# Two small matmul groups on column halves, 512-token projections in the last layer, and a priority for attention tasks in a two-layer hybrid kernel

## The chip, the cores and the metric

The kernel runs on one core of a Trainium2 chip. The metric is the device time of one execution in microseconds. The engines that matter are TensorE (PE; its weight loads are listed as PEld), VectorE (DVE), ScalarE (ACT), GpSimd (POOL) and the queue of SyncE (SP), from which nearly all DMAs are issued.

## The reference

Two layers work on 528 tokens (16 meta tokens ahead of 512 real ones; the reference also has 112 padding rows, which the kernel leaves away). Each layer does:

```
hn   = rmsnorm(h)
proj = hn @ w_in                    # 1024 -> sq sk sv | rq rk rv rg | u
sb   = stick_breaking(sq, sk, sv)   # 6 heads of 64, log-sigmoid and a running sum over the keys
ro   = rmsnorm(retention(rotary(rq), rotary(rk), rv)) * silu(rg)   # 6 heads, chunks of 128, one state
so   = s5_mixer(u)                  # diagonal state space model, then a gated output
h    = h + concat(sb, ro, so) @ w_out
hn   = rmsnorm(h)
h    = h + (silu(hn @ w_gate) * (hn @ w_up)) @ w_down              # 1024 -> 2816 -> 1024
```

Only the 512 real tokens of the last layer are returned. In that layer the meta tokens still act as keys, values and state, but nothing needs their queries (sq, rq) or their gate (rg).

## The kernel before, in words

Activations lie transposed, 128 channels of the partitions by 528 tokens. Every large product is done with operands split into a high and a low part of type fp32r, and three products (high by high, low by high, high by low) added in PSUM. `mm3` (L352) does this: for each of the K tiles of 128 rows and each of the three products one matmul per bank. A PSUM bank takes 512 columns, so 528 tokens go as two banks of 264 columns, and the 512 tokens of the last layer's output projection and MLP (`open_ps`, `spans`) as one bank of 512. The 23 column blocks of `w_in` (three head pairs of each of sq, sk, sv, rq, rk, rv, rg, and two of u) come in the order of the string `PROJ`. In the last layer they are done for all 528 tokens too (`proj`, L1088; `scaled`, L1103, multiplies by the norm on DVE and so empties the banks).

Attention, retention and S5 are small matmuls with long stretches of ACT, DVE and POOL between them. They are written as Python generators, called tasks. `spawn` (L172) puts a task on one list. `mm3` calls `tick` (L191) after each step, and `tick` runs, in the order of the list, up to six tasks whose due time has come and whose resource is free, each up to its next `yield`; a task that has run goes to the end of the list. So the program order of every engine's queue is fixed when the kernel is built. Due times come from `spend` (L96): every operation is charged to its engine by a formula of `Timed` (V, SC and G are DVE, ACT and POOL), for instance 160 + 1.2 x columns ns for a DVE operation with both inputs in SBUF, and a task is due again when its last operation is reckoned done. Waiting tasks hold or wait for resources that are counted in Python too: 6 of the 8 PSUM banks, and 4 of those 6 for attention scores (`take`, `banks`).

- `sb_lane` / `sb_pair` / `sb_group`: stick breaking for one head pair after the other (tiles z, e, sp, hi, lo, av).
- `ret_lane` / `ret_pair` (L955): retention for a head pair: transposes (rtp), the product of keys and values of four chunks (kv), scores (sc), output (ro), then the norm over the head (hsq, hps) and the gate (sg).
- `s5_lane` / `s5_mix` / `s5_glu`: es, scans on DVE, yps, ysm, then the gated product (pj from hi/lo of ysm, glu).
- `s5_params` with `outputs` (L617): builds the matrices of S5, among them the kernel matrix (kps, copied by DVE into tz).
- `Unit.drive`: the split of the next weight block into its two parts (wh on ACT, wl on DVE).

In kv one matmul a chunk forms the 128x128 product of both heads of the pair, of which only the two diagonal 64x64 blocks are read. In kps eight matmuls of two K parts write 32 partitions by 4 x 128 columns.

After the projections the output projection runs in three parts (`OUT_PARTS`): in the first layer stick breaking (mix 0, 1, 2), then S5 (6, 7), then retention (3, 4, 5); in the last layer S5, stick breaking, retention. Ahead of each part `drain` runs tasks alone until the part's inputs are there; inside a part `mm3` ticks the tasks that are left.

Of the kernel before, what the change touches and what calls it, by code (L numbers as in the profile page):

```python
# [12 lines left out]
ALU = mybir.AluOpType  # L13
# [75 lines left out]
def hybrid_kernel(ctx, tc, A, out, dbg=None):  # L89
# [16 lines left out]
    class Timed:  # L106
# [6 lines left out]
        def __getattr__(self, name):  # L113
            f = getattr(self.eng, name)

            def issue(*a, **k):
# [7 lines left out]
                return f(*a, **k)  # L124
            return issue

    V = Timed(nc.vector, "V", {"one": (150, 1.05), "two": (160, 1.2), "tensor_scalar": (150, 0.55),
                               "tensor_tensor_scan": (180, 2.2)})
    SC = Timed(nc.scalar, "SC", {"one": (230, 0.8), "two": (230, 0.8)})
    G = Timed(nc.gpsimd, "G", {"one": (180, 2.1), "two": (180, 2.1), "memset": (100, 0.85)})  # L130
# [1 line left out]
    def mm(out, lhsT, rhs, start, stop, more=False):  # L132

        n = math.prod(out.shape[1:]) / 2.4
        t = 2 * max(109.0, 2 * n + 3) if rhs.dtype == F32 else max(110.0, 1.055 * n + 5)
        spend("PE", t / 2 if 64 in (rhs.shape[0], out.shape[0]) else t)
        nc.tensor.matmul(out, lhsT=lhsT, rhs=rhs, start=start, stop=stop, skip_group_check=more)  # L137
# [31 lines left out]

    tasks = []  # L170

    def spawn(gen, at=0.0):  # L172
        tasks.append([gen, at, None, None, 0.0])

    free = {"bank": BANKS, "scores": ZBANKS, "group": GROUPS}

# [14 lines left out]
    def tick(most=TICKS):  # L191

        done = 0
        for t in list(tasks):
            if done < most and t[1] <= busy["PE"] + LEAD and (t[2] is None or t[2]()):
                tasks.remove(t)
                now[0] = t
                t[3] = None
                try:
                    t[2] = next(t[0])  # L200
                    tasks.append(t)
                except StopIteration:
                    pass
                now[0] = None
                done += 1
        return done
# [139 lines left out]
    def open_ps(nt, s="pj"):  # L346
        return [bank(s), bank(s)] if nt == T else [bank(s)]
# [4 lines left out]
    def mm3(ps, w, x, c0=0, nt=T, first=True, last=True, ticks=TICKS):  # L352

        a, b = w
        xh, xl = x
        kt = len(xh)
        for k in range(kt):
            for i, (wt, xt) in enumerate(((a, xh), (a, xl), (b, xh))):
                for p, (c, n) in zip(ps, spans(nt)):
                    mm(p[:, :n], lhsT=wt[:, k, :], rhs=xt[k][:, c0 + c:c0 + c + n],  # L360
                       start=first and k == 0 and i == 0, stop=last and k == kt - 1 and i == 2)
                tick(ticks)
# [177 lines left out]
    def s5_params(l, engines, scal, par):  # L540
# [76 lines left out]
        def outputs():  # L617

            c_r, c_i = v3(braw[:, 2 * P:3 * P]), v3(braw[:, 3 * P:4 * P])
            for hf in range(2):  # L620
                for ri in range(2):
                    gg[ri, hf] = gp.tile([P, 640], F32, tag="g", name=nm("gg"))
                    G.memset(gg[ri, hf], 0.0)
            for ri in range(2):
                mul, add, sub = on(engines[ri])
                pr, pi = powers(0, 5)
                x1, x2 = (gp.tile([P, 640], F32, tag="g", name=nm("gx")) for _ in range(2))
                mul(v4(x1, 5), wide(c_r, 5), pi if ri else pr)
                mul(v4(x2, 5), wide(c_i, 5), pr if ri else pi)
                yield  # L630
                for q in range(2):
                    r = slice(64 * q, 64 * q + 64)
                    for hf in range(2):
                        o = gg[ri, hf][r, :].rearrange("p (m c) -> p m c", c=32)[:, :, 16 * q:16 * q + 16]
                        a, b = (x[r, 320 * hf:320 * hf + 320].rearrange("p (m c) -> p m c", c=16) for x in (x1, x2))
                        (add if ri else sub)(o, a, b)
                yield
            bbd = [tt("bbd"), tt("bbd")]
            for ri, src in ((0, bbr), (1, bbi)):
                G.memset(bbd[ri][:, :256], 0.0)  # L640
                for q in range(2):
                    engines[ri].tensor_scalar(
                        out=bbd[ri][64 * q:64 * q + 64, :256].rearrange("p (t c) -> p t c", c=32)[:, :, 16 * q:16 * q + 16],
                        in0=src[64 * q:64 * q + 64], scalar1=-1.0 if ri else 1.0, scalar2=None, op0=ALU.mult)
            now[0][1] += 2000 + 10000 * l
            yield
            for hf in range(2):
                yield from banks(1)
                ps = bank("kps")
                for t in range(4):  # L650
                    for ri in range(2):
                        mm(ps[0:32, P * t:P * t + P], lhsT=bbd[ri][:, 32 * (4 * hf + t):32 * (4 * hf + t) + 32],
                           rhs=gg[ri, hf][:, 160 * t:160 * t + P], start=ri == 0, stop=ri == 1)
                tz[hf] = tt("tz")
                G.memset(tz[hf], 0.0)
                yield
                pv = ps.rearrange("p (t c) -> p t c", c=P)
                for j in range(Q):
                    o = tz[hf][96 - 32 * j:128 - 32 * j, :512].rearrange("p (t c) -> p t c", c=P)[:, :, 32 * j:P]
                    V.tensor_copy(out=o, in_=pv[0:32, :, 0:P - 32 * j])  # L660
                yield
                freed(1)
            over.append("outputs")
# [291 lines left out]
    def ret_pair(l, p, q, k, vt, gate, res):  # L955
# [21 lines left out]
        yield from banks(1)  # L977
        ps = bank("kv")
        for j in range(4):
            mm(ps[:, P * j:P * j + P], lhsT=kt[:, P * j:P * j + P], rhs=v[:, P * j:P * j + P], start=True, stop=True)  # L980
        yield
        for hh in range(2):
            r, c = slice(64 * hh, 64 * hh + 64), 64 * hh
# [100 lines left out]
    for l in range(LAYERS):  # L1084
        got = {}
        mix = [None] * 8

        def proj(w):  # L1088
            ps = open_ps(T)
            mm3(ps, w, nrm.x)  # L1090
            return ps

        def two_proj():
# [8 lines left out]

        def scaled(n, ps):  # L1103
            t = tt(n)
            for b, (c, m) in zip(ps, spans(T)):
                V.tensor_tensor(out=t[:, c:c + m], in0=b[:, :m], in1=nrm.rr[:, c:c + m], op=ALU.mult)
            return t

        def after(n, p, t, l=l, got=got, mix=mix):

# [32 lines left out]
            for i in range(2):  # L1143
                mix[6 + i] = yield from slow_split(so[i])

        spawn(s5_lane())
        for p in range(3):
            spawn(sb_lane(p))
        for p in range(3):
            spawn(ret_lane(p))  # L1150
        held = []
        for i, (n, p) in enumerate(proj_order(l)):
            if l == 0 and i < 2:
                if i == 0:
                    first = two_proj()
                held.append((n, p, first[i]))
            else:
                held.append((n, p, proj(weight())))
            if i == HOLD[l]:
                nrm.finish()  # L1160
                if l == 0:
                    spawn(first_params())
            if i >= HOLD[l]:
                for n, p, ps in held:
                    spawn(after(n, p, scaled(n, ps)), busy["V"])
                held = []
        last = l == LAYERS - 1
        c0, nt = (NM, S) if last else (0, T)
# [26 lines left out]
        for n, (kind, i, f0, nf) in enumerate(mlp_order()):  # L1195
# [16 lines left out]
                continue  # L1212
            if n == 3 and not last:
                par = []
                spawn(s5_params(l + 1, (G, G), scal, par), busy["G"])
            a, b = tt("ga"), tt("up")
            for t, ps in ((a, gate), (b, ps)):
                for p, (c, m) in zip(ps, spans(nt)):
# [98 lines left out]
```

## Time and profile before

| | |
|---|---|
| median of 3 runs | 1351.04 us (1349.2 to 1351.19) |
| profiled execution, its own time | 1346.14 us |
| its span, first to last instruction | 1344.4 us |
| mean granted TensorE clock | 0.997 |
| PE / DVE / ACT / POOL busy | 98% / 60% / 44% / 25% |

The span divides into: start and first projections to 56 us; first layer's projections with tasks to 224.8; its output projection, the rest of the tasks among it, to 302; its MLP to 698; the last layer's projections with tasks from there to 918; output projection to 972; MLP to the end. "Busy" of matmuls counts their whole latency, so neighbours overlap: the step from one start to the next is what a matmul costs in a dense stretch. A matmul of plain fp32 shows as two records (two passes).

### The profile page before, as it was taken

Reading aid. Unit: us, or ns where it says so; the run is one execution under the profiler, and the core shown is the slowest. Engines: PE = TensorE matmul, PEld = TensorE weight load, DVE = VectorE, ACT = ScalarE, POOL = GpSimd, SP = SyncE. Lnnn points to the kernel's source line nnn. Section 1 sums busy time; section 2 is a strip of 40 time slices with the busy share of each in tenths; the row PEclk is TensorE's granted clock in tenths of the full one; section 3 lists DMA queues with packets and bytes.
Section 4 is the critical chain, followed back from the end, with each engine's and each line's share of the span. In section 5 each row is a group of like instructions: output and inputs, shape, how many; then the busy total and the mean of one; then the engine's idle time right before and its main releaser. Section 6 shows DMA issues by size and latency. Waiting matters only on the chain.

```text
span 1344.4 us, 22300 instructions
## 1 busy us (share of the span) xinstructions
PE 1316.5 (98%) x9068; PEld 1203.5 (90%) x9068; DVE 800.6 (60%) x1342; ACT 586.8 (44%) x937; POOL 341.6 (25%) x517
## 2 busy tenths in 40 slices
PE   7999999999999999999999999999999999999998
PEld 7998888999999999999999988997888888888886
DVE  8795788776445355534478884645765544553453
ACT  6556445654242133313355657743544422442241
POOL 4590230212999012101212110100122201220120
PEclk9999999999999999999999999999999999999999
DMA  5121222132223222322231321312222332223222
GB/s 191 56 77 59 88 89 72 41 95 102 95 64 95 95 82 92 95 95 82 73 114 64 104 73 39 109 48 95 90 103 94 94 94 95 95 94 98 90 90 98
DMA packets 39126, 118.24 MB, mean 88 GB/s; under 512 B 4976, under 2 KB 5488, under 8 KB 39024
## 3 DMA queue, kind: packets, MB, share of 16 engines
q1 hardware_dynamic: 39024, 116.82, 26.7%
q8 instruction: 71, 1.16, 0.4%
q14 instruction: 31, 0.25, 0.1%
HBM read 111.46 MB, written 2.10 MB: 84 GB/s over the span
## 4 chain that ended last, share of the span: by engine, by line
PE 87%; DVE 6%; POOL 3%; ACT 2%; issue 1%; DMA 1%; SPq 0%; DVEq 0%; POOLq 0%; ACTq 0%
PE pj L137 75%; PE z L137 4%; PE hps L137 2%; PE av L137 1%; PE ro L137 1%; DVE wl L124 1%; ACT e L124 1%; DVE ysm L124 1%; POOL gg L124 1%; PE kps L137 1%; POOL ws L124 1%; PE rtp L143 0%; ACT uc L124 0%; POOL btmp L124 0%; PE kv L137 0%
## 5 line engine op out<-in xcount | busy, mean ns | idle before, releaser
L137 PE MATMUL pj<-xh,wh 128*128 128x264 f32 (+1 forms) x1792 | 454.4, 310 | 15.2 <-ACT wh L124 4.9
L137 PE MATMUL pj<-xl,wh 128*128 128x264 f32 (+1 forms) x1792 | 454.8, 310 | 1.2 <-DVE xl L124 1.2
L137 PE MATMUL pj<-xh,wl 128*128 128x264 f32 (+1 forms) x1792 | 452.4, 309 | 0.3 <-DVE wl L124 0.3
L124 ACT CAST wh<-wr 128x1024 fp32r<-128x1024 f32 (+3 forms) x210 | 205.9, 983 | 384.3 <-PE pj L137 358.4
L124 DVE TENSOR_TENSOR wl<-wr,wh 128x1024 fp32r<-128x1024 f32 (+3 forms) x210 | 292.9, 1395 | 84.9 <-ACT wh L124 82.1
L137 PEld LDWEIGHTS pj<-xh,wh 128*128 128x128 f32 x1792 | 298.2, 190 | 34.7 <-issue 7.3
L137 PEld LDWEIGHTS pj<-xl,wh 128*128 128x128 f32 x1792 | 299.3, 190 | 18.2 <-DVE xl L124 1.4
L137 PEld LDWEIGHTS pj<-xh,wl 128*128 128x128 f32 x1792 | 298.1, 189 | 17.2 <-DVE wl L124 0.5
L137 PE MATMUL pj<-hi,wh 128*128 128x264 f32 (+1 forms) x720 | 193.9, 323 | 0.0
L137 PE MATMUL pj<-lo,wh 128*128 128x264 f32 (+1 forms) x720 | 193.3, 321 | 0.0
L137 PE MATMUL pj<-hi,wl 128*128 128x264 f32 (+1 forms) x720 | 192.8, 321 | 0.1
L124 DVE TENSOR_TENSOR h<-h,pj 128x264 f32<-128x264 f32 (+1 forms) x144 | 69.3, 510 | 137.7 <-PE pj L137 137.5
L124 POOL TENSOR_TENSOR up<-ga,up 128x528 f32<-128x528 f32 (+1 forms) x44 | 60.9, 1385 | 341.2 <-DVE up L124 341.2
L137 PEld LDWEIGHTS pj<-hi,wh 128*128 128x128 f32 x720 | 120.0, 188 | 11.3 <-ACT wh L124 0.8
L137 PEld LDWEIGHTS pj<-hi,wl 128*128 128x128 f32 x720 | 119.9, 188 | 11.1 <-DVE wl L124 0.5
L137 PEld LDWEIGHTS pj<-lo,wh 128*128 128x128 f32 x720 | 119.9, 188 | 10.1
L124 POOL TENSOR_TENSOR lo<-ga,hi 128x528 fp32r<-128x528 f32 (+1 forms) x44 | 59.1, 1342 | 153.6 <-ACT hi L124 153.6
L124 DVE TENSOR_TENSOR up<-pj,R 128x264 f32<-128x264 f32 (+1 forms) x66 | 32.1, 513 | 91.9 <-PE pj L137 91.9
L124 DVE TENSOR_TENSOR ga<-si,up 128x528 f32<-128x528 f32 (+1 forms) x44 | 32.4, 737 | 87.7 <-ACT si L124 56.8
L124 ACT ACTIVATE si<-si,bias 128x528 f32<-128x528 f32 (+1 forms) x44 | 32.1, 730 | 89.8 <-DVE si L124 89.7
L124 ACT ACTIVATE e<-z 128x432 f32<-128x432 f32 (+2 forms) x72 | 37.3, 547 | 43.6 <-PE z L137 43.4
L124 ACT CAST hi<-ga 128x528 fp32r<-128x528 f32 (+1 forms) x44 | 27.6, 627 | 62.2 <-DVE ga L124 62.2
(219 smaller groups left out, 1412.8 us busy)
## 6 DMA issues: line engine op xcount, KB each, us to landing
wr<-in_w_in_dram SPq DMA_DIRECT2D x44, 512.0 KB, 3.5
wr<-in_w_gate_dram SPq DMA_DIRECT2D x44, 512.0 KB, 3.5
wr<-in_w_up_dram SPq DMA_DIRECT2D x44, 512.0 KB, 3.5
wr<-in_w_down_dram SPq DMA_DIRECT2D x32, 512.0 KB, 3.5
wr<-in_w_out_dram SPq DMA_DIRECT2D x16, 384.0 KB, 3.2
wr<-in_w_down_dram SPq DMA_DIRECT2D x16, 384.0 KB, 3.1
rc<-in_rope_dram SPq DMA_DIRECT2D x12, 264.0 KB, 3.7
rs<-in_rope_dram SPq DMA_DIRECT2D x12, 264.0 KB, 3.9
```

The source lines that it names most:

```text
L124: return f(*a, **k)
L137: nc.tensor.matmul(out, lhsT=lhsT, rhs=rhs, start=start, stop=stop, skip_group_check=more)
```

## The change

Five things are changed.

1. kps: the four 32-row results of a half are written to two partition groups (0 to 31 and 64 to 95) by two columns of blocks, and the two groups alternate in program order. The copies to tz are halved in width; DVE does the first group, ACT the second.
2. kv: a matmul for each head, 64 columns of weights and 64 moving columns, on its own half of the array's columns and of the partitions, in place of one for the pair.
3. Last layer: sq, rq and rg (nine blocks) are projected for the 512 real tokens alone, in one bank; POOL sets the 16 meta columns of the tile to zero.
4. Priority: a task has a number, 0 or 1; `tick` goes through the tasks sorted by it. Stick breaking, the work behind sq, sk and sv, and the weight splits have 0; S5, its parameters, retention, and the work behind u, rq, rk, rv and rg have 1. A task that a task spawns has its parent's.
5. The planner's formula for DVE: 1.04 ns in place of 1.2 for a column of an operation with both inputs in SBUF, and 160 + 1.14 x columns for scalar_tensor_tensor.

```diff
-    V = Timed(nc.vector, "V", {"one": (150, 1.05), "two": (160, 1.2), "tensor_scalar": (150, 0.55),
+    V = Timed(nc.vector, "V", {"one": (150, 1.05), "two": (160, 1.04), "scalar_tensor_tensor": (160, 1.14), "tensor_scalar": (150, 0.55),
...
-    def spawn(gen, at=0.0):
-        tasks.append([gen, at, None, None, 0.0])
+    def spawn(gen, at=0.0, pri=None):
+
+        tasks.append([gen, at, None, None, 0.0, now[0][5] if pri is None and now[0] else pri or 0])
...
-        for t in list(tasks):
+        for t in sorted(tasks, key=lambda t: t[5]):
...
-                for t in range(4):
+                for t0 in range(2):
                     for ri in range(2):
-                        mm(ps[0:32, P * t:P * t + P], lhsT=bbd[ri][:, 32 * (4 * hf + t):32 * (4 * hf + t) + 32],
-                           rhs=gg[ri, hf][:, 160 * t:160 * t + P], start=ri == 0, stop=ri == 1)
+                        for b in range(2):
+                            t = 2 * b + t0
+                            mm(ps[64 * b:64 * b + 32, P * t0:P * t0 + P], lhsT=bbd[ri][:, 32 * (4 * hf + t):32 * (4 * hf + t) + 32],
+                               rhs=gg[ri, hf][:, 160 * t:160 * t + P], start=ri == 0, stop=ri == 1)
...
-                    V.tensor_copy(out=o, in_=pv[0:32, :, 0:P - 32 * j])
+                    for b, copy in ((0, V.tensor_copy), (1, SC.copy)):
+                        copy(out=o[:, 2 * b:2 * b + 2], in_=pv[64 * b:64 * b + 32, :, 0:P - 32 * j])
...
-            mm(ps[:, P * j:P * j + P], lhsT=kt[:, P * j:P * j + P], rhs=v[:, P * j:P * j + P], start=True, stop=True)
+            for hh in range(2):
+                c = slice(P * j + 64 * hh, P * j + 64 * hh + 64)
+                mm(ps[64 * hh:64 * hh + 64, c], lhsT=kt[:, c], rhs=v[:, c], start=True, stop=True)
...
-        def proj(w):
-            ps = open_ps(T)
-            mm3(ps, w, nrm.x)
+        def proj(w, c0, nt):
+            ps = open_ps(nt)
+            mm3(ps, w, nrm.x, c0, nt)
...
+            c0, nt = tokens(n)
+            if c0:
+                G.memset(t[:, :c0], 0.0)
+            for b, (c, m) in zip(ps, spans(nt)):
+                V.tensor_tensor(out=t[:, c0 + c:c0 + c + m], in0=b[:, :m], in1=nrm.rr[:, c0 + c:c0 + c + m], op=ALU.mult)
...
+            return (NM, S) if l == LAYERS - 1 and n in ("sq", "rq", "rg") else (0, T)
...
-        spawn(s5_lane())
+        spawn(s5_lane(), pri=1)
         for p in range(3):
             spawn(sb_lane(p))
         for p in range(3):
-            spawn(ret_lane(p))
+            spawn(ret_lane(p), pri=1)
...
-                    spawn(after(n, p, scaled(n, ps)), busy["V"])
+                    spawn(after(n, p, scaled(n, ps)), busy["V"], pri=int(n not in ("sq", "sk", "sv")))
```

The parameters of S5 (`first_params`, and `s5_params` of the next layer) are spawned with pri=1 too.

## Rows read from the trace of the kernel before

**Rows 1.** The page: busy us, share of the span and instructions of each engine.

```profile
PE 1316.5 (98%) x9068; PEld 1203.5 (90%) x9068; DVE 800.6 (60%) x1342; ACT 586.8 (44%) x937; POOL 341.6 (25%) x517
```

**Rows 2.** Busy time by stretch: length, each engine, clock, DMA share, GB/s.

```profile
56.00:273.00 217.00, 207.73 (x1671) 191.89 (x1668) 169.11 (x380) 122.28 (x237) 72.62 (x141) 0.99 0.22 70
150.00:200.00 50.00, 46.21 (x360) 42.58 (x360) 45.56 (x84) 22.99 (x43) 18.62 (x18) 0.97 0.25 75
```

**Rows 3.** PE's waits, 55 to 275 and 700 to 945: total, times, longest.

```profile
PE pj L137 <- DVE rq L124: 2.0, 1, 2.0
PE hps L137 <- ACT hsq L124: 1.8, 1, 1.8
...
PE hps L137 <- ACT hsq L124: 1.3, 1, 1.3
```

**Rows 4.** The chain in order of time: two dense stretches (start, us, passes).

```profile
417.23 286.85 PE pj L137 x2352
...
984.62 333.56 PE pj L137 x1440
```

**Rows 5.** PE's timeline around kps (start, us, count); its weight loads, min/median/max ns.

```profile
98.89 1.94 PE L137 MATMUL kps<-gg,bbd 128*32 128x128 f32 x16
100.75 0.51 PE L137 MATMUL pj<-xh,wl 128*128 128x264 f32 x2
...
L137 PEld LDWEIGHTS kps<-gg,bbd x64: 106/110/110, 98.9 to 416.8; 128*32 128x32 f32 x64
```

**Rows 6.** PE's timeline, matmuls on column halves (128*64) and neighbours; weight loads.

```profile
244.20 0.40 PE L137 MATMUL pj<-hi,wl 128*128 128x264 f32 x2
244.54 1.09 PE L137 MATMUL ro<-sc,rv 128*64 128x128 f32 x14
245.56 0.94 PE L137 MATMUL ro<-rm,st 128*128 128x128 f32 x6
...
114.99 0.49 PE L137 MATMUL av<-e,v 128*64 128x144 f32 x8
115.41 0.49 PE L137 MATMUL hps<-hsq,blk 128*128 128x264 f32 x1
...
233.38 0.20 PEld L137 LDWEIGHTS ro<-sc,rv 128*64 128x64 f32 x4
```

**Rows 7.** PE's timeline around a kv group.

```profile
254.82 1.05 PE L137 MATMUL kv<-rv,kt 128*128 128x128 f32 x8
255.63 0.49 PE L137 MATMUL pj<-hi,wl 128*128 128x264 f32 x2
255.96 0.28 PE L137 MATMUL pj<-hi,wh 128*128 128x264 f32 x1
```

**Rows 8.** DVE by operation and shape: busy us, mean ns, idle before.

```profile
L124 DVE TENSOR_TENSOR wl<-wr,wh 128x1024 fp32r<-128x1024 f32 x164 | 252.3, 1538 | 74.5 <-ACT wh L124 74.4
...
L124 DVE TENSOR_TENSOR ga<-si,up 128x512 f32<-128x512 f32 x22 | 15.2, 692 | 33.5 <-ACT si L124 33.5
```

**Rows 9.** A stretch at the lower clock, columns as in rows 2.

```profile
194.55:197.95 3.40, 3.40 (x18) 3.40 (x17) 3.34 (x7) 0.59 (x1) 0.00 (x0) 0.50 0.24 79
```

**Rows 10.** Timelines of PE and DVE: the S5 lane and the output projection behind it.

```profile
188.50 0.39 PE L137 MATMUL yps<-uc,tz 128*128 128x132 f32 x2
...
208.94 0.39 PE L137 MATMUL yps<-uc,tz 128*128 128x132 f32 x2
...
237.06 0.51 PE L137 MATMUL pj<-hi,wh 128*128 128x264 f32 x2
...
271.46 0.71 DVE L124 TENSOR_TENSOR lo<-glu,hi 128x528 fp32r<-128x528 f32 x1 [2.22 <-ACT hi L124]
...
272.82 0.60 PE L137 MATMUL pj<-hi,wh 128*128 128x264 f32 x2
```

**Rows 11.** POOL from 704 to 941 by operation: busy us, mean ns, idle before; tz copies.

```profile
L124 POOL TENSOR_TENSOR rm<-rq,rc 128x528 f32<-128x528 f32 x3 | 4.0, 1331 | 46.2 <-DVE sc L124 29.9 <-DMA rc<-in_rope_dram 16.3
...
L124 DVE COPY tz<-kps x16: 278/482/685, 100.9 to 425.9; 32x512 f32<-32x512 f32 x4, 32x384 f32<-32x384 f32 x4, 32x256 f32<-32x256 f32 x4, 32x128 f32<-32x128 f32 x4
```

More of the change, by code (lines that the diff above doesn't have):

```diff
@@ L656, in outputs @@
                 yield
-                pv = ps.rearrange("p (t c) -> p t c", c=P)
+                pv = ps[:, :2 * P].rearrange("p (t c) -> p t c", c=P)
                 for j in range(Q):
                     o = tz[hf][96 - 32 * j:128 - 32 * j, :512].rearrange("p (t c) -> p t c", c=P)[:, :, 32 * j:P]
-                    V.tensor_copy(out=o, in_=pv[0:32, :, 0:P - 32 * j])
+                    for b, copy in ((0, V.tensor_copy), (1, SC.copy)):
+                        copy(out=o[:, 2 * b:2 * b + 2], in_=pv[64 * b:64 * b + 32, :, 0:P - 32 * j])
                 yield
@@ L1104, in scaled, with tokens @@
             t = tt(n)
-            for b, (c, m) in zip(ps, spans(T)):
-                V.tensor_tensor(out=t[:, c:c + m], in0=b[:, :m], in1=nrm.rr[:, c:c + m], op=ALU.mult)
-            return t
+            c0, nt = tokens(n)
[3 more added lines that the diff above has]
+                V.tensor_tensor(out=t[:, c0 + c:c0 + c + m], in0=b[:, :m], in1=nrm.rr[:, c0 + c:c0 + c + m], op=ALU.mult)
+            return t
+        def tokens(n, l=l):
+            return (NM, S) if l == LAYERS - 1 and n in ("sq", "rq", "rg") else (0, T)
         def after(n, p, t, l=l, got=got, mix=mix):
@@ L1157, in hybrid_kernel @@
             else:
-                held.append((n, p, proj(weight())))
+                held.append((n, p, proj(weight(), *tokens(n))))
             if i == HOLD[l]:
@@ L1161, in hybrid_kernel @@
                 if l == 0:
-                    spawn(first_params())
+                    spawn(first_params(), pri=1)
             if i >= HOLD[l]:
                 for n, p, ps in held:
-                    spawn(after(n, p, scaled(n, ps)), busy["V"])
+                    spawn(after(n, p, scaled(n, ps)), busy["V"], pri=int(n not in ("sq", "sk", "sv")))
                 held = []
@@ L1214, in hybrid_kernel @@
                 par = []
-                spawn(s5_params(l + 1, (G, G), scal, par), busy["G"])
+                spawn(s5_params(l + 1, (G, G), scal, par), busy["G"], pri=1)
             a, b = tt("ga"), tt("up")
```

## The prediction

> **What bounds the kernel now.** I read the page's busy times first, then the stretches, PE's waits, the chain of work in order of time for the price of one matmul, and the timelines around the operations that change. The page shows PE at 98% of the span, the next engine at 60% [rows 1], so the kernel is bound by the sum of what PE has to stream, and a matmul taken away anywhere in a dense stretch should come off the end, unless the place where it stood waits for something else. Such places are few. In the 217 us in which the first layer's tasks run, PE lacks 217 - 207.73 = 9.3 us [rows 2]; DVE, at 45.56 of 50 us in the tightest part of it, is the engine that runs out there. The longest single waits are for DVE emptying a projection's banks (2.0 us) and, once in each layer, for ACT in the norm behind the last retention pair (1.8 and 1.3 us) [rows 3]. Everything else, the MLPs above all, is a dense stream: 2352 matmuls of 264 columns in 286.85 us, 122.0 ns each, and 1440 of 512 columns in 333.56 us, 231.6 ns each [rows 4].
>
> **Last layer on 512 tokens.** Nine blocks, each 8 K tiles by 3 products, now two matmuls of 264 columns and then one of 512: 216 pairs at 2 x 122.0 = 243.9 ns become 216 at 231.6 ns. 216 x 12.3 ns = 2.65 us off PE. All of it lies in the projections of the last layer, which are dense. DVE empties one bank where it emptied two, which costs it no more. POOL gets nine small memsets, and ACT's square of sq or rq now waits for POOL as well as DVE. The memset would be late if it were queued behind a rotation that waits for its table: those waits are 16.3 us over three, 5.4 us each [rows 11]. A rotation is issued at the end of its head norm, and between it and the next memset another projection of 48 matmuls, 5.9 us, goes by; I take 0, and one hit of 5.4 us as the far end.
>
> **kps.** Four groups of 16 passes (fp32 takes two passes a matmul). One takes 100.75 - 98.89 = 1.86 us [rows 5]. Does the trace show halves of the columns running beside each other? The retention output does it already: 14 passes on alternating halves took 245.56 - 244.54 = 1.02 us [rows 6]. A full-width pass of 128 columns is read from kv: 255.63 - 254.82 = 0.81 us, plus the first projection step behind it, 0.33 us where 0.24 is usual, so 0.90 us for 8, 0.112 us each [rows 7]. Fourteen one after the other would be 1.57 us; seven pairs are 0.78, and the other 0.24 us, with the 0.10 us by which the projection step ahead is long (244.54 - 244.20 = 0.34), are the price of going into this form and out of it: 0.34 us. kps is in a narrow form before and after, so that price stays, and eight passes a group go: 8 x 0.112 x 4 = 3.6 us; I take 3.5. The far end is nothing, if two groups of 32 columns did not overlap as two of 64 do.
>
> The Trainium skill (TensorE: Matmul & The Clock Gate, Part 3: Packing small matmuls) says that a weight load overlaps with running matmuls only where the row group differs; the halves here share all rows, so the rule speaks against both edits. By it a pair would pay its load (0.11 us for kps [rows 5]) and its stream (0.11) in turn, 0.22 us, as much as two passes now, and kps would gain nothing. The trace does not agree: the seven retention pairs, loads included, took 0.146 us each with the price of the form, and four such loads fit into 0.20 us [rows 6]. What the rule would make of the total is among the rivals.
>
> **kv.** Six groups. Eight full passes cost 0.90 us. Afterwards there are 16 passes, eight pairs, of 64 columns, plus the price of the form, 0.34 us, which kv does not pay now. No row has a pair of 64 columns. From above it costs what a pair of 128 does, 0.112; from below, the stick breaking output: two pairs of 144 columns and two of 16 in 115.41 - 114.99 = 0.42 us [rows 6], less 2 x 0.126 for the long ones (0.112 x 144/128) and about 0.1 for leaving the form, leaves 0.03 for a short one. 64 lies midway, so 0.07: 8 x 0.07 + 0.34 = 0.90 us. I take no change; the ends are 8 x 0.03 + 0.34 = 0.58 (1.9 us gained over six) and 8 x 0.112 + 0.34 = 1.24 (2.0 us lost).
>
> **The copies to tz.** Sixteen DVE copies, 482 ns in the median [rows 11], become half as wide, and ACT gets sixteen of its own, at most the same each, up to four in a row: under 2 us in which ACT's queue holds back the next exponential or weight split. ACT is at 44% [rows 1]; I take 0, and 2 us as the far end if PE stood behind one of them.
>
> **The planner.** A DVE operation of 512 columns on two SBUF operands was reckoned at 160 + 1.2 x 512 = 774 ns and is now at 692; measured: 692 [rows 8]. That is exact when DVE runs alone. For the weight split of 1024 columns it goes from 1389 to 1225 ns where the mean is 1538 [rows 8], so the reckoning now falls short by more. The priority changes the order only among tasks due in the same tick, the six that a tick may take, and who gets a free bank or score slot first. Total work is the same. Neither has a row that prices it. At most all 9.3 us of idle could go; I take 0 for the likeliest case and leave the two directions to the rivals.
>
> **The sum.** 2.65 + 3.5 + 0 = 6.1 us. The profiled execution took 1346.14 us (span 1344.4), so it would take 1340.0. The median of the runs shown lies 4.9 us above the profiled one, and I carry that along: 1351.04 - 6.1 = 1344.9, say 1345.
>
> **Rivals.**
>
> A. Attention first pays. Stick breaking is one serial lane, pair after pair; served first, it ends sooner and its ACT and DVE steps lie beside more projections. If half of the 9.3 us goes, with one stretch at the lower clock (0.50 for 3.40 us, 18 matmuls done where 3.40 / 0.122 = 28 fit, so 1.2 us [rows 9]), the time is 1344.9 - 4.6 - 1.2 = 1339. For it: PE's idle is nearly all there. Against: the biggest wait there is for DVE, whose work is not less.
>
> B. The stalls eat the gain. With shorter reckoned times, PE instructions are placed earlier, and PE, which is in order, stands where DVE is late. What is queued behind the waiting instruction is the whole projection stream. Half as much idle again and one more low-clock stretch: 1344.9 + 4.6 + 1.2 = 1350.7, no change. For it: the weight split's mean of 1538 ns against 1225. Against: most operations are now reckoned as measured.
>
> C. S5 comes late, and the kernel is slower. In the first layer the second part of the output projection needs S5. Its last DVE step ended at 271.46 + 0.71 = 272.17, and the part began at 272.82 [rows 10]: it is already what PE waits for. The part ahead of it began at 237.06 and holds only 144 matmuls, 17.6 us. S5 already starves: two neighbouring yps steps stand 20.4 us apart (188.50 and 208.94 [rows 10]) though by the code only eight short DVE operations lie between. With priority 1 it asks for banks after stick breaking; if stick breaking then ends sooner and S5 half such a wait, 10 us, later, each of these microseconds is PE's, and the clock falls at least once: 1344.9 + 12 = 1357. It decides from 6.1 + 2.7 = 8.8 us of delay. Against: stick breaking that ends sooner also frees its four banks sooner, so S5 may catch up. In the last layer S5's blocks come first, and this cannot happen.
>
> D. The halves do not overlap, as the rule above has it. kps gains nothing, kv pays 8 x (0.11 + 0.07) + 0.34 = 1.78 us a group, 5.3 us over six; with the 2.65 us gained: 1351.04 + 2.6 = 1353.7. Rows 6 speak against it.
>
> **Chances and range.** Forecast 0.42, A 0.18, B 0.18, C 0.19, D 0.03. Differences under 0.2%, 2.7 us, cannot be told from no change here. Faster: the forecast but for its slow fringe (0.40), A, and the fast fringe of B: 0.59. Same: the rest of the forecast and most of B: 0.19. Slower: C and D, 0.22. The likeliest case's own range: 1340 to 1349, from kv's two ends (1.9 and 2.0 us), kps at half its gain, and about 3 us of stalls either way. The range for 8 in 10 reaches below A's 1339 and just over C's 1357: 1337 to 1358.
>
> **What would show it.** kps groups of about 1.0 us for 16 passes, that is pairs of starts with a step of 0.11 us from pair to pair. kv groups of 0.8 to 0.9 us. In the last layer 432 matmuls of 264 columns fewer and 216 of 512 more. If kps stays at 1.8 us, or kv goes over 1.2, those steps are wrong. PE's idle in the first layer's tasks near 9 us says that the order did nothing; under 5 us is A, over 13 us B, with waits for DVE; for C, an idle stretch of PE that ends on the DVE step lo<-glu, with stick breaking's last output well before 235 us. A total outside 1340 to 1349 with all PE terms as worked out would mean that the order, which I put at nothing, decides.

## The result and the profile after

The changed kernel takes 1359.62 us (median of 4 runs, 1356.64 to 1362.1) against 1350.88 for the kernel before: ratio 1.0072, interval 1.0059 to 1.0085. It is 0.7% slower, where 0.45% faster was forecast. The profiled execution took 1360.73 us, with a span of 1358.9.

The page after, its busy times and three rows of its 40 slices (compare [rows 1]):

```profile
PE 1321.6 (97%) x8900; PEld 1192.7 (88%) x8900; DVE 794.9 (58%) x1333; ACT 591.8 (44%) x953; POOL 336.6 (25%) x526
...
PE   7999997899999999999999999999999999999998
DVE  8884598577444545544557975555665544554453
...
PEclk9999998699999999999999999999999999999999
```

PE has 168 instructions fewer and yet is busy 5 us longer. One place stands out: in the seventh and eighth slice, about 204 to 272 us, PE's busy share and its clock fall together. The stretches of that place (columns as in [rows 2]):

```profile
215.90:275.70 59.80, 45.45 (x288) 35.92 (x286) 41.35 (x89) 30.55 (x64) 5.52 (x7) 0.71 0.03 10
275.70:324.10 48.40, 48.40 (x398) 48.37 (x397) 38.46 (x75) 26.62 (x42) 6.30 (x4) 1.00 0.27 82
...
228.85:239.09 10.24, 5.69 (x28) 4.36 (x30) 9.80 (x22) 4.24 (x8) 0.00 (x0) 0.50 0.00 0
242.50:266.39 23.89, 18.27 (x83) 15.36 (x84) 12.49 (x28) 12.30 (x25) 1.33 (x1) 0.50 0.00 1
```

The first layer's projections end at 215.9, the output projection begins at 275.7. For 59.8 us PE has only the matmuls of the tasks that are left (288 records), and for 10.24 + 23.89 us of it the granted clock is 0.50, the 1.2 GHz level. Before, the same stretch was 12.3 us long (224.8 to 237.1) at the full clock:

```profile
224.80:237.10 12.30, 11.17 (x96) 8.80 (x94) 11.16 (x23) 6.80 (x14) 2.54 (x2) 1.00 0.48 143
```

By the code the first part of the output projection needs the outputs of stick breaking. Each of them is the tile av (its PE row over that layer, in ns the shortest, median and longest, then the first and the last start; first after, then before):

```profile
L137 PE MATMUL av<-e,v x96: 179/379/717, 88.0 to 271.1; 128*64 128x256 f32 x36, 128*64 128x144 f32 x24, 128*64 128x16 f32 x24, 128*64 128x272 f32 x12
L137 PE MATMUL av<-e,v x96: 179/332/443, 88.1 to 235.7; 128*64 128x256 f32 x36, 128*64 128x144 f32 x24, 128*64 128x16 f32 x24, 128*64 128x272 f32 x12
```

It begins within 0.1 us of where it began before, and its last start is at 271.1 where it was at 235.7. Its split into two parts is done at 272.2; up to 275.7 PE then still has matmuls of retention and S5 that stand ahead in its queue. PE's waits in the first layer, 55 to 290 us (total, times, longest):

```profile
PE z L137 <- DVE lo L124: 4.7, 2, 3.1
PE rtp L143 <- DVE rm L124: 3.9, 1, 3.9
PE pj L137 <- ACT v L124: 2.1, 1, 2.1
PE hps L137 <- DVE lo L124: 1.8, 1, 1.8
```

Three of the four are waits for DVE. The timeline of the longest single one (start, us, engine; in brackets PE's idle time and what ended it):

```profile
231.69 2.31 DVE L124 SCALAR_TENSOR_TENSOR ysm<-u,cols,yps 32x132 f32<-32x132 f32 x5
234.03 0.71 DVE L124 TENSOR_TENSOR rm<-rm,rsw 128x528 f32<-128x528 f32 x1
234.79 1.12 PE L143 MATMUL rtp<-ident,rm 128*128 128x128 f32 x4 [3.87 <-DVE rm L124]
...
235.84 1.79 PE L137 MATMUL av<-e,v 128*64 128x272 f32 x12
```

PE stands at a transpose of retention, for which DVE first does five steps of S5, both of the second rank; queued behind it on PE is av of stick breaking, of the first.

The local edits are visible and pay. PE's timeline at kps, at one kv group each in the first and last layer (compare [rows 5, 7]):

```profile
97.79 1.07 PE L137 MATMUL kps<-gg,bbd 128*32 128x128 f32 x16
98.78 0.39 PE L137 MATMUL pj<-xh,wh 128*128 128x264 f32 x1
...
182.22 0.69 PE L137 MATMUL kv<-rv,kt 128*64 128x64 f32 x16 [1.00 <-DVE rq L124]
182.83 0.49 PE L137 MATMUL hps<-hsq,blk 128*128 128x264 f32 x1
...
937.56 0.69 PE L137 MATMUL kv<-rv,kt 128*64 128x64 f32 x16
938.18 0.50 PE L137 MATMUL pj<-hi,wh 128*128 128x512 f32 x1
```

Sixteen kps passes take 0.99 us where they took 1.86. Sixteen kv passes take 0.61 us and the step behind them about 0.1 more than usual, 0.7 where it was 0.90. The copies to tz now lie on two engines, at half the length (compare [rows 11]):

```profile
L124 DVE COPY tz<-kps x16: 210/314/418, 99.1 to 458.9; 32x256 f32<-32x256 f32 x4, 32x192 f32<-32x192 f32 x4, 32x128 f32<-32x128 f32 x4, 32x64 f32<-32x64 f32 x4
L124 ACT COPY tz<-kps x16: 200/284/366, 99.5 to 459.9; 32x256 f32<-32x256 f32 x4, 32x192 f32<-32x192 f32 x4, 32x128 f32<-32x128 f32 x4, 32x64 f32<-32x64 f32 x4
```

By stage, the lengths of after against before: up to the end of the first layer's output projection +21.9 us, its MLP -2.2, the last layer's projections -4.9, the rest -0.3; together +14.5, the difference of the spans. All of the loss is in the first layer's tasks.

### The profile page after: what moved, and what is told of

Its sections match the earlier page's. It is cut to its first block, busy times and chain, and to the rows that moved or that the text cites. A ratio compares the mean times of both kernels' runs of the same rounds, so it can differ in the third digit from the quotient of the medians.

```text
span 1358.9 us, 21961 instructions
## 1 busy us (share of the span) xinstructions
PE 1321.6 (97%) x8900; PEld 1192.7 (88%) x8900; DVE 794.9 (58%) x1333; ACT 591.8 (44%) x953; POOL 336.6 (25%) x526
## 4 chain that ended last, share of the span: by engine, by line
PE 79%; POOL 10%; DVE 6%; ACT 2%; issue 1%; DMA 1%; SPq 0%; DVEq 0%; ACTq 0%; POOLq 0%
PE pj L137 69%; PE z L137 4%; POOL py L124 2%; PE hps L137 2%; POOL st L124 1%; PE av L137 1%; PE ro L137 1%; POOL gg L124 1%; POOL ws L124 1%; DVE wl L124 1%; DVE ysm L124 1%; POOL phr L124 1%; ACT e L124 1%; POOL lo L124 1%; POOL up L124 1%
## 5 line engine op out<-in xcount | busy, mean ns | idle before, releaser
L137 PE MATMUL pj<-xh,wh 128*128 128x264 f32 (+1 forms) x1720 | 449.3, 315 | 11.6 <-ACT wh L124 5.5
L137 PE MATMUL pj<-xl,wh 128*128 128x264 f32 (+1 forms) x1720 | 449.3, 315 | 1.0 <-DVE xl L124 1.0
L137 PEld LDWEIGHTS pj<-xh,wh 128*128 128x128 f32 x1720 | 287.8, 189 | 32.3 <-ACT wh L124 5.5
L137 PEld LDWEIGHTS pj<-xl,wh 128*128 128x128 f32 x1720 | 288.1, 189 | 20.2 <-DVE xl L124 1.2
L137 PEld LDWEIGHTS pj<-xh,wl 128*128 128x128 f32 x1720 | 287.9, 189 | 20.1 <-DVE wl L124 0.5
L137 PEld LDWEIGHTS pj<-lo,wh 128*128 128x128 f32 x720 | 119.4, 188 | 10.2
L124 POOL TENSOR_TENSOR lo<-ga,hi 128x528 fp32r<-128x528 f32 (+1 forms) x44 | 59.0, 1340 | 153.9 <-ACT hi L124 153.7
L124 ACT CAST hi<-ga 128x528 fp32r<-128x528 f32 (+1 forms) x44 | 27.6, 627 | 62.0 <-DVE ga L124 62.0
L124 ACT ACTIVATE e<-z 128x416 f32<-128x416 f32 (+2 forms) x72 | 37.8, 548 | 30.9 <-PE z L137 30.4
```

## The experiments

The theory: the program order costs the time, reshuffled by the priority and by the formulas, and the work saved is real but small beside it. (In the expectations, theory 1 is the first of the rivals below, theory 2 the priority and 2b the sweep, theory 3 the formulas, 3a by degree and 3b by reshuffling.) The rivals: the tz copies that alternate between DVE and ACT put the tasks out of step; the formulas leave too little slack, by degree; the sweep over a sorted list, taken once, lets S5 and retention take banks ahead of the waiting stick breaking. Ratios are to the kernel before, with their intervals. "Parts" are those of the change.

For most of the kernels one row was worked out from its trace (us): end of the first layer's projections (P), the last start of a stick breaking output av (SB), start and end of the first layer's output projection (O1, O2), and from the start of the span to O2 PE's idle (what the gaps between starts have beyond 330 ns) and the time at the 1.2 GHz level; then the span and the ratio.

| kernel | P | SB | O1 | O2 | idle | 1.2 GHz | span | ratio |
|---|---|---|---|---|---|---|---|---|
| before | 224.8 | 235.7 | 237.1 | 302.2 | 12.3 | 6.8 | 1344.4 | 1 |
| after | 215.9 | 271.1 | 275.7 | 324.1 | 26.9 | 37.5 | 1358.9 | 1.0072 |
| work_alone | 204.1 | 247.8 | 249.3 | 301.7 | 14.9 | 10.2 | 1345.0 | 0.9998 |
| order_alone | 223.3 | 245.4 | 242.6 | 305.3 | 14.5 | 10.2 | 1351.3 | 1.0038 |
| reckoning_alone | 221.6 | 269.2 | 265.9 | 320.9 | 23.8 | 23.9 | 1360.7 | 1.0103 |
| old_reckoning | 212.8 | 248.2 | 251.9 | 304.2 | 14.4 | 10.2 | 1341.1 | 0.9975 |
| no_order | 201.0 | 273.6 | 276.0 | 324.4 | 23.2 | 40.9 | 1364.1 | 1.0153 |
| order_and_reckoning | 235.7 | 255.5 | 259.0 | 312.2 | 14.9 | 17.0 | 1355.6 | 1.0065 |
| copies_alone | 206.9 | 249.7 | 251.2 | 303.5 | 12.9 | 13.6 | 1344.4 | 0.9994 |
| dve_copies | 228.4 | 260.7 | 258.3 | 315.1 | 21.5 | 20.5 | 1348.8 | 1.0023 |
| grouped | 216.3 | 249.6 | 251.4 | 306.3 | 15.6 | 13.6 | 1346.7 | 1.0011 |
| first_again | 214.9 | 247.0 | 243.0 | 325.2 | 21.3 | 37.6 | 1362.2 | 1.0121 |
| grouped_first_again | 238.2 | 222.5 | 238.3 | 300.6 | 12.8 | 0 | 1339.2 | 0.9955 |
| bg_first_again | 229.5 | 212.9 | 229.6 | 296.7 | 7.0 | 3.4 | 1342.8 | 0.9959 |
| two_only | 231.5 | 248.1 | 248.6 | 309.9 | 14.8 | 6.8 | 1358.9 | 1.0086 |
| r_hop300 | 224.7 | 276.8 | 273.8 | 323.6 | 27.6 | 23.9 | 1365.9 | 1.0141 |

In five rows O1 stands ahead of SB, though `sb_pair` emits the matmuls of one av in one go, ahead of the output projection: in reckoning_alone two of the last twenty passes of av start from 265.15, the output projection at 265.88, the other eighteen from 267.55. So the order that runs is not the planner's alone; a later stage of the build moves instructions too, and no run separates the two.

**Copies.** Against the first rival: only the copies split over both engines, in the kernel before, and the changed kernel with all copies on DVE.

```diff
 copies_alone (from before)
-                    V.tensor_copy(out=o, in_=pv[0:32, :, 0:P - 32 * j])
+                    for b, copy in ((0, V.tensor_copy), (1, SC.copy)):
+                        copy(out=o[:, 2 * b:2 * b + 2], in_=pv[0:32, 2 * b:2 * b + 2, 0:P - 32 * j])
 dve_copies (from after)
-                    for b, copy in ((0, V.tensor_copy), (1, SC.copy)):
+                    for b, copy in ((0, V.tensor_copy), (1, V.tensor_copy)):
```

> The kernel before with one edit: each copy from kps to tz is cut into two halves, one on DVE and one on ACT, in turn; the matmuls, the order of the tasks and the planner's formulas are those of before. Theory 1 (the alternation misleads the planner): the planner counts each switch of engine inside a step as a dependence, so eight short copies push DVE's and ACT's reckoned time on, stick breaking of the second pair is placed later, and more of the small matmuls fall behind the last projection of the first layer: in this program 170 of them stand between that projection and the output projection, against 56 before and 174 after the change. Expected about 22 us longer than before, 1365 to 1376 us, with a stretch at the lower clock near 220 to 270 us. Theory 2 (the priority) and theory 3 (the shorter DVE formulas) have nothing here that could act: 1350 to 1352 us.

> The changed kernel with one edit: the half copies that went to ACT stay on DVE. Theory 1: 72 small matmuls stand between the last projection of the first layer and the output projection (174 with ACT), so most of the 22 us lost in the first layer come back: 1343 to 1349 us. Theories 2 and 3: priority and formulas are still there, so the loss stays: 1356 to 1362 us.

The split alone costs nothing: 1346.33 us, 0.9994 (0.9979 to 1.001), where theory 1 had 1365 to 1376. Taking it out of the changed kernel brings 1350.7, 1.0023 (1.0004 to 1.0042), between what the theories expected, so most of the loss goes there; but what does no harm by itself is not the cause by itself. The copies are one more number that reshuffles the order.

**Parts taken singly and in pairs.** Work (parts 1 to 3), priority (4) and formulas (5).

```diff
 reckoning_alone (from before; order_and_reckoning and no_order have it too)
-    V = Timed(nc.vector, "V", {"one": (150, 1.05), "two": (160, 1.2), ...
+    V = Timed(nc.vector, "V", {"one": (150, 1.05), "two": (160, 1.04), "scalar_tensor_tensor": (160, 1.14), ...
 order_alone (from before; old_reckoning has it with the work)
-        for t in list(tasks):
+        for t in sorted(tasks, key=lambda t: t[5]):
 work_alone (from after): both lines as before
```

> The kernel before with the priority alone (tasks sorted, no halves, 528 tokens, old formulas). Theory 1: no loss from the order, 44 small matmuls between the last projection and the output projection against 56 before: 1345 to 1353 us. Theory 2 (a waiting stick breaking task stands ahead in the sweep, the task that frees the bank runs later in it, and a task of priority 1 behind that one takes the bank): stick breaking later by 20 us, 1358 to 1372 us.

> The kernel before with the two new DVE formulas alone. Theory 1: not the cause; 1347 to 1354 us. Theory 3: DVE's shorter reckoned times let steps bunch up; 108 small matmuls stand between the last projection and the output projection against 56 before, at the changed kernel's rate of loss (22 us for 118 more) 10 us: 1357 to 1365 us.

> The kernel before with the three changes of work alone: kps and kv on column halves (with the copies split over DVE and ACT) and the last layer's sq, rq, rg on 512 tokens; order of tasks and DVE formulas as before. If the formulas and the order are what costs, and the work saves what its matmuls save (kps 3.5, projections 2.65, kv about 1.5 by the changed kernel's trace): 7 us less than before, 1339 to 1344 us against 1348. If the work itself costs in the first layer: 1350 to 1362.

> The changed kernel without the sorting (work and formulas, tasks in the order of the list). Theory 3 (formulas): the loss stays or grows, 1356 to 1366 us; 252 small matmuls stand behind the last projection of the first layer here, 174 in the changed kernel. Theory 2 (order): the loss goes, 1341 to 1348.

> The changed kernel with the old DVE formulas (work and order). Theory 3: the formulas' 13.7 us go and the work's 7 us stay, the order's 5 us too: 1343 to 1350 us. Theory 2: no better than the changed kernel, 1356 to 1362.

> The kernel before with order and formulas, without the work. If effects add: 5 + 13.7 us over before, 1364 to 1370. If what counts is when stick breaking ends: 95 small matmuls stand behind the last projection here (108 with the formulas alone, 44 with the order alone), so it lies between the two, 1351 to 1361 us.

Measured, as per cent against the kernel before:

| | formulas old | formulas new | the formulas' share |
|---|---|---|---|
| nothing else | 0 | +1.03 (0.75 to 1.32) | +1.03 |
| work | -0.02 (-0.15 to 0.11) | +1.53 (1.25 to 1.81) | +1.55 |
| priority | +0.38 (0.25 to 0.51) | +0.65 (0.43 to 0.87) | +0.27 |
| work and priority | -0.25 (-0.38 to -0.13) | +0.72 (0.59 to 0.85) | +0.97 |

The formulas cost in all four pairs, 0.95 on average, though with the priority alone the two intervals overlap. They change no operation, only the times by which the planner lays out the program, so what costs is the order, and with it who gets a bank when. The priority is worth +0.38, -0.23, -0.38 and -0.81: it is not what makes the kernel slow. Without the formulas the change is faster than the kernel before, 1343.71 us. Two stretches of the trace of the worst single part, columns as before:

```profile
221.60:265.90 44.30, 31.02 (x156) 24.72 (x155) 24.66 (x48) 25.63 (x55) 4.42 (x4) 0.73 0.11 31
265.90:320.90 55.00, 55.00 (x465) 53.57 (x462) 40.66 (x81) 28.67 (x46) 6.67 (x4) 1.00 0.25 73
```

These are reckoning_alone: no work saved, no priority, and the same picture as after, a stretch of 44.3 us behind the projections with 156 matmul records at a mean clock of 0.73, and stick breaking's last output at 269.2. With the old formulas (old_reckoning) that stretch is:

```profile
212.80:251.90 39.10, 30.64 (x233) 25.11 (x231) 31.03 (x71) 24.98 (x51) 5.48 (x7) 0.87 0.05 14
251.90:304.20 52.30, 52.30 (x433) 51.85 (x433) 40.67 (x79) 28.65 (x46) 6.72 (x4) 1.00 0.26 77
```

It is still long, but it starts earlier; its output projection is over at 304.2. The work by itself gains nothing (work_alone, 1347.4 us; 1339 to 1344 was expected if the saved work arrived, 1350 to 1362 if the work itself cost). Its trace shows where the gain goes: the MLP of the first layer is 1.5 us shorter, but the last layer's projections take 222.9 us where they took 219.8, with 4.0 us of PE idle against 2.2 and 6.8 us at 1.2 GHz against none.

**Last layer's part alone.** The first layer's program stays that of before.

```diff
-                held.append((n, p, proj(weight())))
+                held.append((n, p, proj(weight(), *tokens(n))))
```

> The kernel before with sq, rq, rg of the last layer on 512 tokens and nothing else; the first layer's program is that of before. 216 steps of two matmuls of 264 columns become one of 512: 2.65 us less in the last layer's projections, 1345 to 1347 us against 1348, if the planner's order there is not made worse; the last layer's stretch from its first projection to its last 217.2 us against 219.8. If the new order costs there: 219 us or more and no gain.

1351.2 us, 1.0025 (1.0011 to 1.004): slower, where 2.65 us were to be saved. O2 is at 301.7, as before. The first layer's MLP is 3.2 us longer, one wait of 2.7 us for DVE's wl among it, and the last layer's projections are 2.0 us longer, with PE waits of 1.8 us for stick breaking's lo and 1.4 for rq and 3.4 us at 1.2 GHz; the kernel before has one wait of 1.6 there, for ysm, and none at that level. So here too the order took more than the work gave.

**The dose.** The formula's slope for two SBUF operands alone, 1.2 in the kernel before.

```diff
-    V = Timed(nc.vector, "V", {"one": (150, 1.05), "two": (160, 1.2), ...
+    V = Timed(nc.vector, "V", {"one": (150, 1.05), "two": (160, 1.28), ...     (1.24, 1.12, 1.04 in l124, l112, two_only)
 r_hop300 (from reckoning_alone)
-HOP = 200
+HOP = 300
```

> The kernel before with a longer DVE formula, 1.28 ns a column in place of 1.2 (the change went to 1.04, which alone cost 13.7 us). Theory 3a (shorter reckoned times issue steps too early and PE stands behind them): longer times cannot do that, 1344 to 1351 us. Theory 3b (the times themselves do not matter; any shift reorders who gets banks, and the kernel before stands at a good place of it): 124 small matmuls stand behind the last projection, as bad as the shorter formula's 108, stick breaking ends at 255 to 270 us, and the time is 1353 to 1364 us.

> The kernel before with 1.24 ns a column, a little longer than its 1.2. Theory 3a: no loss, 1346 to 1350 us. Theory 3b (85 small matmuls behind the last projection): may cost as any other shift, 1349 to 1356.

> The kernel before with 1.12 ns a column for DVE operations on two SBUF operands, halfway from 1.2 to 1.04, and no formula of its own for scalar_tensor_tensor. Theory 3a (shorter reckoned times cost by degree): about half of the 13.7 us, 1352 to 1358 us. Theory 3b (reshuffling; 67 small matmuls stand behind the last projection against 56 before): anywhere, by that count 1346 to 1352.

> The kernel before with 1.04 ns a column and without the second new formula (scalar_tensor_tensor on SBUF operands then also goes by 1.04). Theory 3a: at least the loss of both formulas together, 1358 to 1364 us. Theory 3b (76 small matmuls behind the last projection, 108 with both formulas): much less, 1347 to 1354.

> The kernel before with both new formulas and a pause of 300 ns in place of 200 between a task's steps, which gives back the 85 ns that an operation of 528 columns lost. Theory 3a: most of the loss comes back, 1346 to 1352 us. Theory 3b (146 small matmuls behind the last projection): as slow as with the formulas alone or slower, 1356 to 1368.

From 1.28 down: 1.0009 (0.9993 to 1.0025), 0.9976 (0.9963 to 0.9988), 1, 1.0005 (0.9987 to 1.0023), 1.0086 (1.0063 to 1.0109). It is flat within a quarter of a per cent, and then one value is 0.86% off: at 1.12, half the step, a cost by degree would have shown half of the loss, and none is there. HOP is the time that the planner adds behind every operation, of any engine, before the task may go on; 100 ns more of it with the new formulas gave 1.0141 (1.0119 to 1.0164), no faster than without (1.0103), where too little slack would have been cured. So a loss in proportion to the slack taken away falls. Reshuffling does not come out clean either: it expected a loss at 1.28 and little at 1.04, and there the theory by degree was right (l128, two_only; l124 lies under both ranges). A threshold between 1.12 and 1.04 is not excluded. In two_only the loss is not in one place: O2 +7.7, the first layer's MLP +4.3, the last layer's projections +3.7.

**The sweep.** By a count in the planned order of the changed kernel (no trace shows who holds a bank), scores of the second head pair wait for banks while tasks of the second rank take them, since a bank that comes free in a sweep goes to whoever stands behind in the list. So the sweep was begun anew after each task, with and without the tz copies grouped by engine, four for DVE and then four for ACT.

```diff
 first_again
-        for t in sorted(tasks, key=lambda t: t[5]):
-            if done < most and ...
+        while done < most:
+            for t in sorted(tasks, key=lambda t: t[5]):
+                if id(t) not in seen and ...: break
+            else:
+                break
...
 grouped (bg_first_again also orders s5_mix's copies by (t + j) % 2)
-                for j in range(Q):
-                    for b, copy in ((0, V.tensor_copy), (1, SC.copy)):
+                for b, copy in ((0, V.tensor_copy), (1, SC.copy)):
+                    for j in range(Q):
```

> The changed kernel with the sweep that begins again after each task, and nothing else (the half copies still alternate). If the priority inversion in the sweep is the larger part of the loss, stick breaking ends ahead of 250 us and the time is 1341 to 1347 us; if the grouping of the copies was what helped in the kernel with both, it stays at 1354 to 1361. 113 small matmuls stand behind the last projection of the first layer (174 in the changed kernel, 0 with both).

> The changed kernel with the half copies to tz issued DVE's four first, then ACT's four, and nothing else. If grouping is what brings the gain of the kernel with both edits: 1339 to 1346 us. If reshuffling is all there is, no gain is promised: its program has 131 small matmuls behind the last projection (174 in the changed kernel, 0 with both edits), and I expect it between the two, 1347 to 1360 us.

> The changed kernel with two edits of the planner: after each task the sweep begins again at the first task that can go on, so a freed bank goes to the waiting task of the lowest number and not to the next in the sweep; and the half copies to tz are issued DVE's first, then ACT's. Theory 2b (in the sorted sweep a waiting score task stands ahead of the task that frees its banks, and one of priority 1 behind takes them; six times between the second and third score group of the second pair in the changed kernel's plan, once here): stick breaking ends inside the projections (no small matmul stands between the last projection and the output projection), the drain is gone and the work's gain shows: 1337 to 1343 us. If lateness of stick breaking is not what costs: 1350 to 1360.

> As the kernel with the new sweep and the grouped copies to tz, and the sixteen copies of S5's input u are grouped by engine too. Stick breaking's stages end 30 to 60 projection matmuls earlier in the program than without that. Once it ends ahead of the point from which it costs (about 249 us in the kernels so far) nothing more is to be had there: 1338 to 1343 us, like the kernel without this edit. If earlier is still better: 1333 to 1338.

The sweep alone made it worse: 1364.14 us, 1.0121 (1.0082 to 1.016), slower than either expectation. Grouping alone 1351.06, 1.0011 (0.9995 to 1.0027). Both together 1341.03, 0.9955 (0.994 to 0.997), the fastest kernel of the study, and with the copies of S5's input grouped too 1342.83, 0.9959 (0.9944 to 0.9973). The two edits do not add up: a good order came of both, not a cure of a cause. The two stretches of first_again show that another lane can be the late one (first the drain, then the output projection; then DVE's last S5 step):

```profile
214.90:243.00 28.10, 25.07 (x192) 20.50 (x190) 27.34 (x60) 14.99 (x31) 5.47 (x4) 1.00 0.11 29
243.00:325.20 82.20, 74.29 (x553) 69.37 (x552) 60.94 (x113) 43.02 (x74) 15.12 (x13) 0.85 0.23 65
...
292.78 1.33 DVE L124 TENSOR_TENSOR lo<-glu,hi 128x528 fp32r<-128x528 f32 x2 [3.77 <-ACT hi L124]
```

Stick breaking ends at 247.0, but S5's last step ends at 294.1, 22 us later than in the kernel before [rows 10]. The output projection has to wait for it, from 282.7, where the part ahead ends, to 293.8, where S5's begins, and takes 82.2 us. That is rival C's mechanism, in another kernel than the one it was put forward for. In the fastest kernel stick breaking is not late: its last output, at 222.5, lies ahead of the projections' end. S5 still is: its part begins at 271.3, 8.3 us behind the end of the part ahead (5.8 us in the kernel before).

```profile
56.00:238.30 182.30, 176.81 (x1441) 161.60 (x1441) 141.00 (x325) 102.23 (x200) 62.94 (x131) 1.00 0.22 68
238.30:300.60 62.30, 58.29 (x490) 56.32 (x489) 53.65 (x101) 36.94 (x62) 14.28 (x12) 1.00 0.28 82
```

**What the runs settle, and what stays open.** Shown: the order in which the program is laid out is what costs. In four pairs of kernels that differ in the formulas alone the new formulas draw the slower order, in three of them clear of noise; but not in every order, for with them in place dve_copies (1.0023), grouped (1.0011) and grouped_first_again (0.9955) lose little or nothing against the kernel before. In the changed kernel the loss lies where a lane outlives the projections that PE could do beside it. Over the table, where stick breaking ends by 250 us the output projection ends between 296.7 and 306.3, but for two_only (309.9) and first_again, whose S5 is late; where it ends later, at 255.5, 260.7, 269.2, 271.1, 273.6 and 276.8, O2 follows: 312.2, 315.1, 320.9, 324.1, 324.4, 323.6. That goes together over the kernels; no run moves stick breaking alone. Nor is it the only place: in order_alone, two_only and tokens_alone the first layer's MLP is longer too, by 4.4, 4.3 and 3.2 us.

Open: why these reckoned numbers draw a late lane, which numbers make a good order, and what the later stage of the build adds. The number of small matmuls left behind the last projection does not say it; copies_alone has 170 and loses nothing, the changed kernel 174 and loses 22 us there.

## Why the prediction was wrong

It was the planner's step that failed: "Neither has a row that prices it. [...] I take 0". The order was put at nothing without a row, and it took all of the gain and more. The formulas, which were thought exact for most operations, cost 0.95% on average, 13 us, twice the 6.1 us that the rest was to save; with the old ones the changed kernel is 4.5 us faster than the kernel before (0.9975). The terms of the work, too, came off the end only where the order let them: work_alone saves nothing, and tokens_alone is slower. The step asked whether single operations are reckoned as measured; it should have asked what becomes of a program order that was found with the old numbers. The rivals had the directions, but not the size: B's 4.6 us more idle and one more stretch at the lower clock stand against 14.6 us more idle (26.9 against 12.3; counted as in [rows 2], stretch less busy time, 20.9 against 9.3) and 30.7 us more at 1.2 GHz.

- **Last layer on 512 tokens**, -2.65 us: right. The last layer's projections are 4.9 us shorter; besides these 2.65 about 1.8 are PE idle (0.4 us for 2.2) and about 0.5 are kv. Alone, the part's gain was lost to the order.
- **kps**, -3.5 us: right. 0.99 us for 16 passes where "about 1.0 us" was named, four groups, 4 x (1.86 - 0.99) = 3.5. Rival D falls. The rule of the Trainium skill (TensorE: Matmul & The Clock Gate, Part 3: Packing small matmuls), that a load overlaps only where the row group differs, does not hold for these column halves: by it nothing would have been gained.
- **kv**, 0: the sign was open, and it gained some. A pair of 64 columns takes 0.058 us from start to start, where 0.07 was taken, and the price of the form was 0.24, not 0.34: 8 x 0.058 + 0.24 = 0.70 us against 0.90, 1.2 us over six groups, if all were alike, inside the stated ends. They are not quite: in the last layer one group stands in two pieces and one among the matmuls of av.
- **tz copies**, 0: right as a price of their own (copies_alone), but they move the order of the changed kernel by half a per cent (dve_copies).
- **Memset**, 0: in the last layer's projections of the changed kernel no wait of PE over 0.15 us shows, and none of ACT's waits is for POOL.
- **Rival A**: the priority was worth -0.81 to +0.38%, depending on the rest. In grouped_first_again, where stick breaking ends 13 us sooner, the time is 7.2 us under the kernel before, where A had 12, and some 6 of these are the work saved.
- **Rival B** had its sign right: idle "over 13 us", "with waits for DVE". Its reason, that shorter reckoned times place PE's instructions too early, is not borne out as a matter of degree (l112, r_hop300), though l128 and two_only fit it.
- **Rival C** gave 1357, near the time measured, but by another lane: it has stick breaking early and S5 late, and here stick breaking is late by 35 us though it has the priority. S5's last step is late as well (289.7 against 272.2), but its part follows the one ahead at 294.8 without a gap, so PE does not wait for it.
- What the prediction named for its own failure, a total outside 1340 to 1349 with the PE terms as worked out, so that the order "decides", is what happened.

How much of the 21.9 us the lower clock took is argued, not measured: 14.6 us are idle and about 2 us of work were saved, which leaves some 9 us beside 30.7 us at the lower level. Steps stretched by that level count in part as idle here, so the division is rough.

## What to carry to other kernels

Where program order comes out of a planner's reckoned times, every edit of those times, of an operation's engine or of its length can draw a new order. Here such draws lay between 0.9955 and 1.0153, far wider than the work that was saved (0.5%), though some edits moved nothing (copies_alone, l112, l128). Change the work and the planner separately, run each, and take the best order by measurement, not the one whose formulas are the most exact. Read a bad one first at the place where the dense filler ends, and look for the lane that ends last behind it.

## What the runs showed of the hardware

Matmuls on two column halves with the same rows run beside each other also at 64 columns: the second of a kv pair starts 6 to 8 ns after the first, and a pair takes 58 to 59 ns. Two groups of 32 columns do so too (kps: 6 to 7 ns, a pair 109). Entering the form costs a longer first step (100 ns where 51 follow; in kps 127 where 102 follow).

In the changed kernel the granted clock fell to 0.50 at 228.85, when PE had started nothing between 227.70 and 229.54, came back at 239.09 for 3.4 us, and was at 0.50 again until 266.39. So the drain was paid twice: by the waits, and by the slower matmuls between them.
